# Layer 1's experts in a two-layer trunk: outputs added into DRAM by accumulating DMA, token rows taken for two experts by one f32 product, freed memory as weight slots

## The chip, the core and the metric

One core of one Trainium2 chip runs the whole program in one launch. The metric is the device time of an execution in microseconds (us), as the median of several. PE is TensorE, DVE VectorE, ACT ScalarE, POOL GpSimd, SP SyncE; a "record" is one matmul instruction as the profile counts it.

## The reference, cut to what matters

The program is a two-layer backbone for 256 latent tokens (and 256 context tokens, which layer 1 no longer updates) of width 1024. Each layer is a mixer and then a mixture of 16 experts; every token goes to 2 of them. The change is in layer 1's mixture (`need_ctx` is false there):

```python
y = merge(...)                                  # mixer, ends with @ w_out
x = x + m[:, :, 2] * y
h = rms_norm(x, norm2_g) * (1 + m[:, :, 4]) + m[:, :, 3]
g_logits = tf @ router_g                        # 4 groups, then 2 of 4 experts in the best group
...
for e in range(MOE_EXPERTS):                    # 16
    hid = jax.nn.silu(t @ w1[e]) * (t @ w3[e])  # 1024 -> 512
    out = out + gate[:, e:e + 1] * (hid @ w2[e])
x = x + m[:, :, 5] * out                        # the kernel's output
```

All of it is float32. The weights of one expert are w1 and w3 (1024 x 512 each) and w2 (512 x 1024): 6.3 MB.

## The kernel before, in words

**Weight stream.** Every weight goes through a chain of pieces of up to 1 MB (128 partitions x 2048 f32) on SP's DMA queue. `sources` fixes their order; layer 1's mixture has 96 pieces, "four of w1 and w3 of the next expert, two of w2 of this one". A piece lands in a slot of 8 KB per partition. `ws.take` hands the next piece to the compute code, `ws.done` gives its slot back, and `pump` (L159) at once issues the next load into a free slot; the load waits on SP until the last reader of that slot is done, and what comes later on SP waits behind it. `ws.add` turns free memory into slots wherever the program lets memory go. A separate chain for the modulation weights (`in_modw`) shares SP.

**Before the experts.** `finish` computes the end of the mixer: `out_half` (its matmuls are L331 to L333) gives x by column quarters, and a call-back `last` runs, for each quarter, `scaled` (L1300, x times the row A2, which is loaded at L469 on ACT's DMA queue from a small DRAM tensor `md`), `squares`, `logits` (transposes L1317, router products L1323) and `keep`, which splits the scaled row h into three bf16 parts (L1308 on ACT, L1310 on DVE or POOL). `halve` and `swap` give memory of the mixer to the slots. `moe` makes the routing: `rk` (a token's place in its expert's list), the gates `VAL` and the root mean square factor `rs`, both split in three bf16 parts.

**The experts, `experts_sum`.** Every expert has 64 places for tokens. `prepare(e)` makes the one-hot matrix of tokens by places and takes the expert's rows out of the 256 tokens: 48 bf16 matmuls (L1701: 8 blocks of columns, 2 tiles of tokens, 3 parts), 6 more for the row factor (L1693), and a DVE product and sum (L1704, L1706); it also turns the one-hots (L1708) and takes the gates (L1711). `first(e)` is the product with w1 and w3 (L1728, 64 records, two halves of the columns side by side in the PE array) and the SwiGLU; `second(e)` transposes the result (L1742), multiplies it with w2 (L1752, 16 records) and with the gates (L1758). The result y is split in two parts in bf16-like precision (L1761 on ACT, L1762 on DVE), and after every second expert 8 matmuls (L1767) add the rows of both experts back to their tokens, into four PSUM banks `acc` that hold the 256 x 1024 output all the time; they were seeded with x (L1684). The order of the program is prepare(e+1), first(e), second(e-1). At the end ACT and DVE copy `acc` out (L1782) and four DMAs store it (L1783). If an expert has over 64 tokens, `overflow` does the rest; it is a branch that these inputs don't take.

Layer 0's mixture has a piece that matters here: `scatter` (L1488) adds rows of y to rows of the DRAM tensor `yd` by an indirect DMA with addition, issued on POOL.

Of the kernel before, what the change touches and what calls it, by code (L numbers as in the profile page):

```python
# [16 lines left out]
P = 128  # L17
# [11 lines left out]
def _col_layout():  # L29
    off = 0  # L30
    for name, n in (("g1", 16), ("lcw", 16), ("lcb", 4), ("lba", 8), ("lbx", 8), ("lam", 8),
# [13 lines left out]
       "hot16": (1262, 16), "slot": (1278, 128), "dvc": (1406, 4)}  # L45
NMSK = 1410
# [205 lines left out]
class Trunk:  # L252
    def __init__(self, tc, I, out, es, dbg):
# [6 lines left out]
        self.es, self.wp, self.rp = es, ExitStack(), ExitStack()  # L260
# [100 lines left out]
    def setup(self):  # L361
# [894 lines left out]
    def finish(self, l, mix):  # L1256
# [24 lines left out]
        hb = F.get(2, 3, D, dt=BF) if ns == 1 else None  # L1281
        if ns == 2:

            H, self.hd = [F.get(2, D) for s in range(2)], self.dp.tile([4 * P, D], F32, name=f"hd{l}")
# [9 lines left out]
        hR = Ring(F, HR, 2, 256) if ns == 1 else None  # L1294
        wait, kept = ([], [], [], []), {}

        def scaled(c, s):
            sl = slice(256 * c, 256 * c + 256)
            h = kept[c, s] = hR() if ns == 1 else H[s][:, :, sl]
            nc.vector.tensor_tensor(h, self.X[s][:, :, sl], A2[:, s, sl].rearrange("p (o c) -> p o c", o=1)  # L1300
                                    .to_broadcast([P, 2, 256]), op=OP.mult)
# [30 lines left out]
        def last(c, s):  # L1332
            for i, f in enumerate((scaled, squares, logits, keep)):
# [6 lines left out]
        for i, f in enumerate((scaled, squares, logits, keep)):  # L1340
            for cs in wait[i]:
                f(*cs)
        F.free(*self.gates, junk, hfR, *([hR] if hR else []), rts, self.rt, A2)
# [10 lines left out]
        self.moe(l, H if ns == 2 else hb, lg)  # L1354
# [14 lines left out]
    def moe(self, l, hd, lg):  # L1369
# [85 lines left out]
        RV, r = F.get(nt, 3, dt=BF), [G_, T(1)[:, :, 0]]  # L1455
        for i in range(3):
            g_, s_ = (G, rs) if i == 0 else r
            nc.vector.tensor_copy(VAL[:, :, :, i], g_)
            if ns == 1:
                nc.vector.tensor_copy(RV[:, :, i], s_)  # L1460
            if i < 2:
                tt(r[0], g_, VAL[:, :, :, i], op=OP.subtract)
                if ns == 1:
                    tt(r[1], s_, RV[:, :, i], op=OP.subtract)
# [6 lines left out]
        else:  # L1471
            self.experts_sum(l, nt, hd, rk, G, VAL, RV, mxi)
            F.free(hd)
        F.free(rk, G, VAL, RV, rs, mxi)
# [190 lines left out]
    def experts_sum(self, l, nt, hb, rk, G, VAL, RV, mxi):  # L1665


        nc, I, F, R = self.nc, self.I, self.F, self.R
        G2 = F.get(2, 512)
        for o in range(2):  # L1670
            for c in range(2):
                r = slice(64 * (c ^ o), 64 * (c ^ o) + 64)
                nc.scalar.dma_start(G2[r, o], self.md[l, 2][0, c, 1:2].to_broadcast([64, 512]))
        ohR = Ring(F, 2, nt, P, dt=BF)
        gtR, xR, rsR = Ring(F, 3, 1), Ring(F, 2, KC, 64), Ring(F, 2, 64)
# [374 lines left out]
```

## Time and profile before

| | |
|---|---|
| time, median of 3 runs | 1256.99 us (1256.77 to 1258.33) |
| the profiled execution: its own time | 1263.97 us |
| its span in the trace | 1262.2 us |
| PE busy | 1109.3 us, 88% of the span |
| DVE, ACT, POOL busy | 806.6, 560.0, 340.6 us |
| DMA moved | 317.09 MB, mean 251 GB/s |

Times inside the program are us from the span's start. The experts of layer 1 take the last fifth, from about 1016 on. In the tables of stretches a row gives the length, busy time of PE, PEld (weight loads), DVE, ACT and POOL with their instructions, the granted clock of TensorE as a share of 2.4 GHz, the busy share of the 16 DMA engines and the rate in GB/s.

### The profile page before, as it was taken

To read this page: it belongs to the slowest core of one execution; us is meant where nothing else is said; L and a number is where in the kernel's file an instruction comes from. 1 tells how busy PE (TensorE), PEld (TensorE's weight loads), DVE (VectorE), ACT (ScalarE), POOL (GpSimd) and SP (SyncE) were. 2 spreads that over 40 slices of the span, in tenths; PEclk is the share of its full clock that TensorE was granted. 3 is DMA by queue.
4 is the path that set the end of the run, shared out by engine and by line. 5 is a ranking of instruction groups with operands and counts; after the bars stand their busy time and mean duration, and the time that the engine had idled before them with its cause. 6 is when DMAs were issued, how large, how long until landed. Compare 5 with 4: busy or idle time off the path is not lost. (4 is left out here: it accounts for less than half of the span.)

```text
span 1262.2 us, 18733 instructions
## 1 busy us (share of the span) xinstructions
PE 1109.3 (88%) x7206; PEld 780.4 (62%) x7206; DVE 806.6 (64%) x1376; ACT 560.0 (44%) x893; POOL 340.6 (27%) x214
## 2 busy tenths in 40 slices
PE   3998899999919999999999779988998599999996
PEld 1656665666717777777777356655777365555553
DVE  3576836555639999999898646998387533333232
ACT  3355525333417787887886323343353311111111
POOL 1331422233213444444532211344423200000000
PEclk9998988899959999999999888999998899999999
DMA  9663568266386999999983154343476789999960
GB/s 355 215 207 124 172 191 278 71 239 242 114 238 241 352 353 346 364 362 358 356 312 118 71 143 179 117 134 107 149 273 249 282 315 422 424 423 424 416 277 35
DMA packets 74977, 317.09 MB, mean 251 GB/s; under 512 B 20074, under 2 KB 26314, under 8 KB 46080
## 3 DMA queue, kind: packets, MB, share of 16 engines
q1 hardware_dynamic: 54656, 294.10, 61.4%
q0 software_dynamic: 4896, 10.20, 3.6%
q10 hardware_dynamic: 15328, 11.50, 3.3%
q8 instruction: 60, 0.98, 0.3%
q14 instruction: 37, 0.30, 0.1%
HBM read 310.74 MB, written 14.76 MB: 258 GB/s over the span
## 5 line engine op out<-in xcount | busy, mean ns | idle before, releaser
L322 ACT CAST arena_rw<-arena_f 128x1024 fp32r<-128x1024 f32 x256 | 265.1, 1050 | 177.7 <-PE b L333 111.3
L325 DVE TENSOR_TENSOR arena_rw<-arena_f,arena_rw 128x1024 fp32r<-128x1024 f32 x198 | 260.4, 1357 | 81.5 <-ACT arena_rw L322 80.9
L331 PE MATMUL b<-arena_rw,arena_rr 128*128 128x512 f32 (+1 forms) x736 | 275.1, 375 | 2.7 <-ACT arena_rr L1214 1.2
L332 PE MATMUL b<-arena_rw,arena_rr 128*128 128x512 f32 (+1 forms) x736 | 272.0, 370 | 0.0
L333 PE MATMUL b<-arena_rw,arena_rr 128*128 128x512 f32 (+1 forms) x736 | 270.1, 369 | 0.5 <-DVE arena_rr L1215 0.5
L325 POOL TENSOR_TENSOR arena_rw<-arena_f,arena_rw 128x1024 fp32r<-128x1024 f32 x58 | 144.4, 2490 | 235.8 <-ACT arena_rw L322 220.6
L331 PEld LDWEIGHTS b<-arena_rw,arena_rr 128*128 128x128 f32 x736 | 140.5, 191 | 37.9 <-issue 10.6
L333 PEld LDWEIGHTS b<-arena_rw,arena_rr 128*128 128x128 f32 x736 | 140.0, 191 | 25.6 <-issue 3.3
L332 PEld LDWEIGHTS b<-arena_rw,arena_rr 128*128 128x128 f32 x736 | 140.7, 191 | 21.2 <-issue 1.3
L417 PE MATMUL b<-arena_f,cs 128*32 128x256 f32 x768 | 70.2, 420 | 22.2 <-DMA arena_f<-in_modw 22.0
L331 PE MATMUL b<-arena_rr,arena_rw 128*128 128x512 f32 (+1 forms) x192 | 74.4, 391 | 2.7 <-ACT arena_rw L322 1.4
L1728 PE MATMUL b<-arena_f 128*64 128x256 f32 x656 | 76.0, 381 | 0.0
L333 PE MATMUL b<-arena_rr,arena_rw 128*128 128x512 f32 (+1 forms) x192 | 72.3, 380 | 4.1 <-DVE arena_rw L325 4.1
L332 PE MATMUL b<-arena_rr,arena_rw 128*128 128x512 f32 (+1 forms) x192 | 73.6, 384 | 1.0 <-POOL arena_rr L507 1.0
L1728 PEld LDWEIGHTS b<-arena_f 128*64 128x64 f32 x656 | 46.5, 137 | 24.2 <-issue 2.3
L417 PEld LDWEIGHTS b<-arena_f,cs 128*32 128x32 f32 x768 | 20.8, 113 | 56.3 <-issue 26.8
L1761 ACT CAST arena_rr<-arena_f 64x512 fp32r<-64x512 f32 x32 | 19.8, 618 | 69.7 <-DVE arena_f L1758 69.3
L1733 ACT ACTIVATE arena_f<-b 128x256 f32<-128x256 f32 x16 | 6.2, 385 | 98.0 <-PE b L1728 98.0
L331 PEld LDWEIGHTS b<-arena_rr,arena_rw 128*128 128x128 f32 x192 | 36.7, 192 | 18.2 <-issue 7.4
L1744 DVE COPY arena_f<-b 128x256 f32<-128x256 f32 x16 | 6.8, 424 | 64.1 <-PE b L1742 64.0
L1488 POOL DMA_INDIRECT yd<-arena_f x14 | 33.5, 2390 | 50.5 <-ACT arena_f L1578 50.5
L553 POOL TENSOR_TENSOR arena_f<-arena_f 128x512 f32<-128x512 f32 x21 | 30.5, 1458 | 57.1 <-DVE arena_f L550 54.8
(386 smaller groups left out, 1798.2 us busy)
## 6 DMA issues: line engine op xcount, KB each, us to landing
arena_f<-in_moe SPq DMA_DIRECT2D x192, 1024.0 KB
arena_f<-in_modw SPq DMA_DIRECT2D x96, 512.0 KB
arena_f<-in_wod SPq DMA_DIRECT2D x18, 1024.0 KB
arena_f<-in_wev SPq DMA_DIRECT2D x14, 1024.0 KB
arena_f<-md ACTq DMA_DIRECT2D x8, 512.0 KB
arena_f<-in_tok SPq DMA_DIRECT2D x4, 512.0 KB
yd<-arena_f SPq DMA_DIRECT2D x4, 512.0 KB
hd<-md ACTq DMA_DIRECT2D x4, 512.0 KB
```

Source lines behind the costliest of these rows:

```text
L322: nc.scalar.copy(h, raw)
L325: eng.tensor_tensor(l, raw, h.bitcast(F32), op=OP.subtract)
L331: nc.tensor.matmul(ps, ah, bh, start=first, stop=False)
L332: nc.tensor.matmul(ps, ah, bl, start=False, stop=False)
L333: nc.tensor.matmul(ps, al, bh, start=False, stop=last)
L417: nc.tensor.matmul(acc[32 * i:32 * i + 32, 0:256], self.cs[:, k, :], raw[:, i * 256:(i + 1) * 256], start=(k == 0), stop=(k == KC - 1))
L553: (nc.vector if last and c == 3 else nc.gpsimd).tensor_tensor(xs, xs, tmp, op=OP.add)
L1488: self.nc.gpsimd.indirect_dma_start(out=yd[:, :], out_offset=bass.IndirectOffsetOnAxis(ap=dst, axis=0), in_=y, in_offset=None, bounds_chec ...
L1728: nc.tensor.matmul(p[64 * c:64 * c + 64, 256 * w:256 * w + 256], x[:, 4 * b + k], raw[:, 512 * k + 256 * c:512 * k + 256 * c + 256], start ...
L1733: nc.scalar.activation(u, p[:, 0:256], AF.Tanh, scale=0.5)
L1744: nc.vector.tensor_copy(ut, ps[:, 0:256].rearrange("p (b c) -> p b c", b=2))
L1761: nc.scalar.copy(yh[r, c], y[r])
```

## The change

`experts_sum` is written anew:

- The output is no longer gathered in PSUM. x goes to `out` by two DMAs ahead of the experts (L1662, ACT's queue); then each expert's y (128 half rows of 512 f32, 2 KB each) is added into `out`, seen as 512 half rows, by one accumulating indirect DMA on POOL (`scatter`, now L1479). The places' destinations and gates come from `rows(e)`: four bf16 matmuls with 2 or 3 columns (L1681, L1683) and two small DVE instructions.
- `take(j)` takes the rows of experts 2j and 2j+1 with one f32 one-hot, already multiplied by the row factor: 4 DVE instructions build it (L1694), 16 f32 matmuls of 128x128x128 (L1700, two records each) make x for both, and 2 DVE instructions add the shift (L1702). H stays whole in f32: `keep`, its bf16 parts, `RV`, L1693, L1704, L1708, the split of y and L1761, L1762, L1767, L1684, L1782 and L1783 are gone.
- `first` is cut in two around w1 and w3, and `hidden(e-1)` (the transposes), `take` and `rows` stand in between. The copy of the transposes goes from DVE to ACT.
- Memory: without the bf16 parts one more slot is added at the start of `finish`; `swap` also closes `rr2` and gives 2 slots (`F4`); the PSUM-side buffers in `RW` are gone; X[0] is freed as soon as it is copied to `out`. Followed through the program, the largest number of slots in layer 1's mixture goes from 16 to 19. Each load into memory that was X[0] has to wait for the DMAs of L1662.

```diff
+        self.vi2 = cp.tile([P, 4, 2], BF, name="vi2")
+        nc.gpsimd.tensor_tensor(self.vi2, self.vi, self.vi, op=OP.add)
         self.ss, junk = F.get(4, 2), F.get(512, dt=BF)
-        hb = F.get(2, 3, D, dt=BF) if ns == 1 else None
+        H = [F.get(2, D) for s in range(ns)]
...
-        def keep(c, s):
-            sl, h = slice(256 * c, 256 * c + 256), kept.pop((c, s))
-            if ns == 2:
-                return
-            for i in range(3):
-                nc.scalar.copy(hb[:, :, i, sl], h)
-                if i < 2:
-                    (nc.gpsimd if HP[c] else nc.vector).tensor_tensor(h, h, hb[:, :, i, sl], op=OP.subtract)
...
     def halve(self):
         self.rp.close()
-        self.R = self.arena(self.es, "rr2", NR // 2, F32R, "right")
         self.F3 = self.arena(self.es, "f3", NR // 2, F32, "right")
+        self.R = self.arena(self.rq, "rr2", NR // 2, F32R, "right")
         self.ws.add(NR // 4096, self.F3)
     def swap(self):
+        self.rq.close()
+        self.F4 = self.arena(self.es, "f4", NR // 2, F32, "right")
+        self.ws.add(NR // 4096, self.F4)
         self.wp.close()
         self.F2 = self.arena(self.es, "f2", 2048 * NHL)
         self.ws.add(NHL, self.F2)
...
-    def experts_sum(self, l, nt, hb, rk, G, VAL, RV, mxi):
...
+    def experts_sum(self, l, nt, H, rk, rs, G, VAL, mxi):
+        nc, I, F = self.nc, self.I, self.F
+        half = self.out.rearrange("t (c d) -> (t c) d", c=2)
+        for t in range(nt):
+            nc.scalar.dma_start(self.out[t * P:(t + 1) * P, :], self.x(t))
+        G2 = F.get(512)
+        for c in range(2):
+            nc.scalar.dma_start(G2[64 * c:64 * c + 64], self.md[l, 2][0, c, 1:2].to_broadcast([64, 512]))
+        ohR, phR = Ring(F, 3, nt, P, dt=BF), Ring(F, 2, nt, P)
+        gtR, ddR, xR = Ring(F, 6, 1), Ring(F, 6, 1, dt=I32), Ring(F, 2, KC, P)
-        uR, utR, yR = Ring(F, 2, 256), Ring(F, 2, 2, P), Ring(F, 2, 512)
-        sR, yhR, ylR = Ring(R, 2, 2, nt * P), Ring(R, 1, 2, 512), Ring(R, 1, 2, 512)
+        uR, utR, yR = Ring(F, 2, 256), Ring(F, 2, 2, P), Ring(F, 3, 512)
+        F.free(self.X[0])
-        acc = [[self.bank("a") for c in range(2)] for t in range(nt)]
-        for t in range(nt):
-            for c in range(2):
-                nc.tensor.matmul(acc[t][c], self.ident, self.x(t)[:, 512 * c:512 * c + 512], start=True, stop=False)
-        st = {}
-        def prepare(e):
...
             for t in range(nt):
-                for i in range(3):
-                    nc.tensor.matmul(tb[:, 320:384], RV[:, t, i:i + 1].to_broadcast([P, P]), oh[:, t, 0:64],
-                                     start=(t == 0 and i == 0), stop=(t == nt - 1 and i == 2))
-            rr = rsR()
-            nc.scalar.copy(rr, tb[:, 320:384])
-            ps = self.bank()
-            for k in range(KC):
-                for t in range(nt):
-                    for i in range(3):
-                        nc.tensor.matmul(ps[:, 64 * k:64 * k + 64], hb[:, t, i, k * P:(k + 1) * P], oh[:, t, 0:64],
-                                         start=(t == 0 and i == 0), stop=(t == nt - 1 and i == 2))
-            x = xR()
-            nc.vector.tensor_tensor(x, ps.rearrange("p (k t) -> p k t", k=KC),
-                                    rr.rearrange("p (o t) -> p o t", o=1).to_broadcast([P, KC, 64]), op=OP.mult)
-            nc.vector.tensor_tensor(x, x, shift.to_broadcast([P, KC, 64]), op=OP.add)
...
+        st, xs, us = {}, {}, {}
+        def rows(e):
             oh = ohR()
             self.one_hot(oh, "slot", rk, e)
             tb = self.bank()
             for t in range(nt):
+                nc.tensor.matmul(tb[:, 0:2], oh[:, t], self.vi2[:, t], start=(t == 0), stop=(t == nt - 1))
             for t in range(nt):
+                nc.tensor.matmul(tb[:, 2:5], oh[:, t], VAL[:, t, e], start=(t == 0), stop=(t == nt - 1))
+            gt, dst = gtR(), ddR()
+            nc.vector.tensor_scalar(dst, tb[:, 0:1], tb[:, 1:2], self.msk("dsc"), op0=OP.add, op1=OP.add)
+            nc.vector.tensor_reduce(gt, tb[:, 2:5], AX.X, OP.add)
+            st[e] = gt, dst
+        def take(j):
+            ph, x = phR(), xR()
             for t in range(nt):
+                for o in range(2):
+                    nc.vector.tensor_scalar(ph[:, t, 64 * o:64 * o + 64], self.msk("slot")[:, 0:64],
+                                            rk[:, t, 2 * j + o:2 * j + o + 1], rs[:, t:t + 1], op0=OP.is_equal, op1=OP.mult)
+            for b in range(2):
+                ps = self.bank()
+                for k in range(4):
+                    for t in range(nt):
+                        nc.tensor.matmul(ps[:, k * P:(k + 1) * P], H[:, t, (4 * b + k) * P:(4 * b + k + 1) * P], ph[:, t],
+                                         start=(t == 0), stop=(t == nt - 1))
+                nc.vector.tensor_tensor(x[:, 4 * b:4 * b + 4], ps.rearrange("p (k t) -> p k t", k=4),
+                                        shift[:, 4 * b:4 * b + 4].to_broadcast([P, 4, P]), op=OP.add)
+            xs[2 * j], xs[2 * j + 1] = x[:, :, 0:64], x[:, :, 64:128]
...
+                if w == 0:
+                    u = uR()
+                    nc.scalar.activation(u, p[:, 0:256], AF.Tanh, scale=0.5)
+                    nc.vector.scalar_tensor_tensor(u, u, 1.0, p[:, 0:256], op0=OP.add, op1=OP.mult)
+                yield
...
+        def hidden(e):
+            u, ps, ut = us[e], self.bank(), utR()
             for b in range(2):
                 nc.tensor.transpose(ps[:, b * P:(b + 1) * P], u[:, b * P:(b + 1) * P], self.ident)
-            ut = utR()
-            nc.vector.tensor_copy(ut, ps[:, 0:256].rearrange("p (b c) -> p b c", b=2))
-            py = self.bank("m")
+            nc.scalar.copy(ut, ps[:, 0:256].rearrange("p (b c) -> p b c", b=2))
+            us[e] = ut
...
             y = yR()
-            yh, yl = yhR(), ylR()
-            nc.vector.scalar_tensor_tensor(y, py, gt, G2[:, e % 2], op0=OP.mult, op1=OP.mult)
-            for i in range(2):
-                r, c = slice(64 * i, 64 * i + 64), i ^ e % 2
-                nc.scalar.copy(yh[r, c], y[r])
-                nc.vector.tensor_tensor(yl[r, c], y[r], yh[r, c].bitcast(F32), op=OP.subtract)
-            if e % 2:
-                for i, part in enumerate((yh, yl)):
-                    for t in range(nt):
-                        for c in range(2):
-                            nc.tensor.matmul(acc[t][c], S[:, c, t * P:(t + 1) * P], part[:, c], start=False,
-                                             stop=(e == NE - 1 and i == 1))
-        prepare(0)
+            nc.vector.scalar_tensor_tensor(y, py, gt, G2, op0=OP.mult, op1=OP.mult)
+            self.scatter(half, y, dst)
+        take(0)
+        rows(0)
         for e in range(NE + 1):
-            if e < NE - 1:
-                prepare(e + 1)
-            if e < NE:
-                first(e)
+            f = first(e) if e < NE else iter(())
+            next(f, None)
+            if e:
+                hidden(e - 1)
+            if e % 2 and e < NE - 1:
+                take(e // 2 + 1)
+            if e + 1 < NE:
+                rows(e + 1)
+            run_all(f)
             if e:
                 second(e - 1)
-        F.free(ohR, gtR, xR, rsR, uR, utR, yR, G2)
-        for t in range(nt):
-            for c in range(2):
-                sl = slice(512 * c, 512 * c + 512)
-                (nc.vector.tensor_copy if c else nc.scalar.copy)(self.x(t)[:, sl], acc[t][c])
-                (nc.sync if c else nc.scalar).dma_start(self.out[t * P:(t + 1) * P, sl], self.x(t)[:, sl])
-        R.free(sR, yhR, ylR)
+        F.free(ohR, phR, gtR, ddR, xR, uR, utR, yR, G2)
...
+    put("dsc", 2 * BIG + k // 64)
```

In the rows below, one of PE, of before, in the loop (expert 2): `arena_f` is the common f32 memory of tokens, one-hots and weight slots, `b_...` a PSUM bank, the last word the shape of the output and "x8" the number of equal rows. Left of the arrow is what is written.

```order
L1693 MATMUL b_8360<-arena_f 128x64
L1708 LDWEIGHTS arena_f
L1708 MATMUL b_8360<-bfs,arena_f 128x128
L1752 MATMUL b_8335<-arena_f_6980,arena_f 64x512 x4
L1752 MATMUL b_8335<-arena_f_7550,arena_f 64x512 x4
L1701 LDWEIGHTS arena_f
L1701 MATMUL b_8368<-arena_f 128x64
```

Of the changed kernel, PE at the first pass of the loop, from the end of w1 of expert 0:

```order
L1714 MATMUL b_7694<-arena_f 64x256 x11
L1729 MATMUL b_7715<-mskt,arena_f 128x128 x2
L1700 MATMUL b_7723<-arena_f 128x128 x8
L1700 MATMUL b_7733<-arena_f 128x128 x8
L1681 LDWEIGHTS arena_f
L1681 MATMUL b_7744<-vi_99,arena_f 128x2
```

and, a few rows on, from the end of `rows(1)` to the start of expert 2:

```order
L1683 MATMUL b_7744<-arena_f 128x3
L1714 MATMUL b_7694<-arena_f 64x256 x16
L1741 MATMUL b_7770<-arena_f 64x512 x8
L1714 MATMUL b_7785<-arena_f 64x256 x8
L1714 MATMUL b_7785<-arena_f_6978,arena_f 64x256 x8
L1729 MATMUL b_7806<-mskt,arena_f 128x128 x2
```

Between L1742's turn and w2 stood 48 bf16 products per expert and now none; ahead of w3 stand 16 f32 products for two experts.

On SP, the loads in the last part of layer 1's mixer, of before (`in_wod` are pieces of the mixer's weights, `in_modw` of the modulation, `in_moe` of layer 1's experts):

```order
L159 DMA arena_f<-in_modw 128x1024 x2
L159 DMA arena_f<-in_wod 128x2048
L159 DMA arena_f<-in_modw 128x1024 x2
L159 DMA arena_f<-in_wod 128x2048
L159 DMA arena_f<-in_modw 128x1024
L159 DMA arena_f<-in_wod 128x2048
L159 DMA arena_f<-in_modw 128x1024
L159 DMA arena_f_6980<-in_wod 128x2048
L159 DMA arena_f<-in_modw 128x1024
L159 DMA arena_f_6980<-in_moe 128x2048
```

and the same place now:

```order
L159 DMA arena_f<-in_modw 128x1024
L159 DMA arena_f<-in_moe 128x2048
L159 DMA arena_f<-in_modw 128x1024
L159 DMA arena_f<-in_wod 128x2048
L159 DMA arena_f<-in_modw 128x1024 x2
L159 DMA arena_f<-in_wod 128x2048
L159 DMA arena_f<-in_moe 128x2048
L159 DMA arena_f<-in_modw 128x1024
L159 DMA arena_f<-in_wod 128x2048
L159 DMA arena_f<-in_modw 128x1024
L159 DMA arena_f_6978<-in_wod 128x2048
```

Two pieces of the experts moved ahead of the last mixer pieces; the order inside each chain is the same.

On POOL, which had nothing to do in layer 1's experts before, the first of the 16 scatters (512x512 is `out` as half rows), with the semaphores that each waits for (DMASW... is that of an earlier scatter, DMAHW... of a load or store of a hardware queue):

```order
L1479 DMA out<-arena_f 512x512 [waits DMAHW1_49,DMAHW3_49,DMAHW0_49,DVE_49]
L1479 DMA out<-arena_f 512x512 [waits DMASW2_49,DMASW3_49,DVE_49,Activation_49]
L1479 DMA out<-arena_f 512x512 [waits DMASW3_49,DVE_49,Activation_49]
L1479 DMA out<-arena_f 512x512 [waits DMASW5_49,DMASW4_49,DVE_49]
L1479 DMA out<-arena_f 512x512 [waits DMASW5_49,DVE_49]
```

Each scatter waits for the one before it to have landed and for DVE's product with the gates.

## Rows read from the trace of the kernel before

**Rows 1.** Busy time by stretch: the experts, and PE after the weights.
```profile
1020.00:1220.00 200.00, 191.96 (x2018) 113.62 (x2016) 63.33 (x117) 35.48 (x93) 0.00 (x0) 1.00 1.01 418
1220.00:1255.00 35.00, 31.24 (x200) 15.48 (x196) 12.32 (x21) 6.28 (x12) 0.00 (x0) 1.00 0.03 14
```

**Rows 2.** Chain that ended last, in the experts: start, duration, what.
```profile
1016.57 7.06 PE b L1728 x64
...
1081.64 0.73 PE b L1767 x2
1082.45 1.49 PE b L1767 x6
...
1092.48 3.58 PE b L1752 x16
1096.07 1.51 PE b L1701 x48
...
1111.07 0.73 PE b L1767 x2
...
1250.98 0.76 DVE arena_f L1758
...
1252.49 2.08 PE b L1767 x7
```

**Rows 3.** Waits of SP's queue, 1020 to 1221: total us, times, longest.
```profile
SPq L159 <- PE b L1728: 101.7, 42, 5.7
```

**Rows 4.** Groups by line, one pair of experts (1081.64 to 1111.07): busy, mean ns, idle.
```profile
L1742 PE MATMUL b<-mskt,arena_f 128*128 128x128 f32 x4 | 0.9, 300 | 0.0
L1708 PE MATMUL b<-bfs,arena_f 128*128 128x128 bf16 x4 | 0.9, 218 | 0.7 <-ACT arena_f L1696 0.7
L1693 PE MATMUL b<-arena_f 128*128 128x64 bf16 x12 | 0.7, 193 | 0.0
L1711 PE MATMUL b<-arena_f 128*128 128x1 bf16 x12 | 0.6, 164 | 0.0
```

**Rows 5.** The same chain in the mixer: 8 f32 products of 128x128x128.
```profile
902.71 1.78 PE b L1168 x16
```

**Rows 6.** Layer 0's scatters on POOL: duration, first and last start, landing.
```profile
L1488 POOL DMA_INDIRECT yd<-arena_f x14: 1897/2504/2527, 412.1 to 661.6; - x14
DMA to landing us min/median/max: 6.6/11.2/11.5
```

**Rows 7.** DMA queues, 560 to 640, four scatters and four gathers: packets, MB, share.
```profile
DMA packets 4874, 28.84 MB, mean 361 GB/s; under 512 B 1056, under 2 KB 1056, under 8 KB 1658
q0 software_dynamic: 1253, 2.47, 13.4%
```

**Rows 8.** Loads on SP's queue ahead of A2's, by time: start, us, count.
```profile
972.70 2.41 SPq L159 DMA_DIRECT2D arena_f<-in_moe  x5
```

**Rows 9.** The same chain, from A2's load to the first expert.
```profile
974.98 13.05 DMA arena_f<-md
...
1000.22 2.58 PE b L1684 x6
...
1011.36 2.57 PE b L1701 x48
```

**Rows 10.** Waits of SP's queue, 960 to 1020.
```profile
SPq L159 <- PE b L333: 21.9, 1, 21.9
```

**Rows 11.** Busy time by stretch, around the routing.
```profile
974.00:988.00 14.00, 8.98 (x74) 8.57 (x72) 2.31 (x7) 1.62 (x5) 2.24 (x2) 0.97 0.98 393
988.00:998.00 10.00, 4.89 (x24) 4.08 (x25) 5.56 (x9) 5.42 (x12) 5.88 (x4) 0.52 0.05 21
998.00:1013.50 15.50, 8.90 (x85) 5.37 (x84) 12.31 (x65) 6.83 (x17) 0.07 (x1) 0.81 1.00 372
1013.50:1019.50 6.00, 5.84 (x106) 4.77 (x105) 3.25 (x6) 1.91 (x7) 0.00 (x0) 0.91 0.05 10
```

**Rows 12.** Waits of SP's queue at the end, after its last store.
```profile
SPq L1835 <- SPq L1835: 4.2, 2, 3.6
```

**Rows 13.** SP's and ACT's last stores, by time: start, us, count.
```profile
1254.89 0.91 SPq L1783 DMA_DIRECT2D out<-arena_f  x2
1255.21 2.27 ACTq L1783 DMA_DIRECT2D out<-arena_f  x2
```

More of the change, by code (lines that the diff above doesn't have):

```diff
@@ L44 @@
        "colm": (937, 64), "pidx": (1001, 1), "cneg": (1002, 128), "cnegT": (1130, 128), "hot4": (1258, 4),
-       "hot16": (1262, 16), "slot": (1278, 128), "dvc": (1406, 4)}
-NMSK = 1410
+       "hot16": (1262, 16), "slot": (1278, 128), "dvc": (1406, 4), "dsc": (1410, 1)}
+NMSK = 1411
 class Arena:
@@ L1279, in finish @@
         self.ss, junk = F.get(4, 2), F.get(512, dt=BF)
-        hb = F.get(2, 3, D, dt=BF) if ns == 1 else None
+        H = [F.get(2, D) for s in range(ns)]
         if ns == 2:
-            H, self.hd = [F.get(2, D) for s in range(2)], self.dp.tile([4 * P, D], F32, name=f"hd{l}")
+            self.hd = self.dp.tile([4 * P, D], F32, name=f"hd{l}")
             for s in range(2):
@@ L1332, in last @@
         def last(c, s):
-            for i, f in enumerate((scaled, squares, logits, keep)):
+            for i, f in enumerate((scaled, squares, logits)):
                 wait[i].append((c, s))
@@ L1339, in finish @@
         run_all(self.out_half(l, 1, mix, ns, last))
-        for i, f in enumerate((scaled, squares, logits, keep)):
+        for i, f in enumerate((scaled, squares, logits)):
             for cs in wait[i]:
                 f(*cs)
-        F.free(*self.gates, junk, hfR, *([hR] if hR else []), rts, self.rt, A2)
+        F.free(*self.gates, junk, hfR, rts, self.rt, A2)
         self.R.free(*mix)
@@ L1471, in moe @@
         else:
-            self.experts_sum(l, nt, hd, rk, G, VAL, RV, mxi)
-            F.free(hd)
-        F.free(rk, G, VAL, RV, rs, mxi)
+            self.experts_sum(l, nt, hd[0], rk, rs, G, VAL, mxi)
+            F.free(hd[0])
+        F.free(rk, G, VAL, rs, mxi)
     def one_hot(self, out, name, rk, e):
@@ L1703, in prepare @@
-            x = xR()
-            nc.vector.tensor_tensor(x, ps.rearrange("p (k t) -> p k t", k=KC),
-                                    rr.rearrange("p (o t) -> p o t", o=1).to_broadcast([P, KC, 64]), op=OP.mult)
-            nc.vector.tensor_tensor(x, x, shift.to_broadcast([P, KC, 64]), op=OP.add)
-            for t in range(nt):
-                nc.tensor.matmul(tb[:, t * P:(t + 1) * P], oh[:, t], self.identb, start=True, stop=True)
-            for t in range(nt):
-                for i in range(3):
-                    nc.tensor.matmul(tb[:, 256:257], oh[:, t], VAL[:, t, e, i:i + 1], start=(t == 0 and i == 0),
-                                     stop=(t == nt - 1 and i == 2))
@@ L1786, in xt @@
         def xt(xT, ohb, oh, cols):
-            ps, rr = self.bank(), F.get(P)
+            ph = F.get(nt, P)
             for t in range(nt):
-                for i in range(3):
-                    nc.tensor.matmul(ps[:, 0:P], RV[:, t, i:i + 1].to_broadcast([P, P]), ohb[:, t],
-                                     start=(t == 0 and i == 0), stop=(t == nt - 1 and i == 2))
-            nc.scalar.copy(rr, ps[:, 0:P])
+                nc.vector.tensor_scalar(ph[:, t], oh[:, t], rs[:, t:t + 1], None, op0=OP.mult)
@@ L1796, in xt @@
                     for t in range(nt):
-                        for i in range(3):
-                            nc.tensor.matmul(ps[:, k * P:(k + 1) * P], hb[:, t, i, (4 * b + k) * P:(4 * b + k + 1) * P],
-                                             ohb[:, t], start=(t == 0 and i == 0), stop=(t == nt - 1 and i == 2))
-                xb = xT[:, 4 * b:4 * b + 4]
-                nc.vector.tensor_tensor(xb, ps.rearrange("p (k t) -> p k t", k=4),
-                                        rr.rearrange("p (o t) -> p o t", o=1).to_broadcast([P, 4, P]), op=OP.mult)
-                nc.vector.tensor_tensor(xb, xb, shift[:, 4 * b:4 * b + 4].to_broadcast([P, 4, P]), op=OP.add)
-            F.free(rr)
+                        nc.tensor.matmul(ps[:, k * P:(k + 1) * P], H[:, t, (4 * b + k) * P:(4 * b + k + 1) * P], ph[:, t],
+                                         start=(t == 0), stop=(t == nt - 1))
+                nc.vector.tensor_tensor(xT[:, 4 * b:4 * b + 4], ps.rearrange("p (k t) -> p k t", k=4),
+                                        shift[:, 4 * b:4 * b + 4].to_broadcast([P, 4, P]), op=OP.add)
+            F.free(ph)
         def put(y, oh, cols):
-            G2, S = F.get(D), F.get(nt, P)
+            G2, pd, dst = F.get(D), self.bank(), F.get(1, dt=I32)
             self.mod_row(G2, l, 5, 0)
-            ps = self.bank()
             for t in range(nt):
-                nc.tensor.transpose(ps[:, t * P:(t + 1) * P], oh[:, t], self.ident)
-            nc.vector.tensor_copy(S, ps[:, 0:nt * P].rearrange("p (t c) -> p t c", t=nt))
-            for c in range(2):
-                sl = slice(512 * c, 512 * c + 512)
-                nc.vector.tensor_tensor(y[:, sl], y[:, sl], G2[:, sl], op=OP.mult)
-                for t in range(nt):
-                    ps = self.bank()
-                    nc.tensor.matmul(ps, S[:, t], y[:, sl], start=True, stop=True)
-                    nc.vector.tensor_tensor(self.x(t)[:, sl], self.x(t)[:, sl], ps, op=OP.add)
-            F.free(G2, S)
+                nc.tensor.matmul(pd[:, 0:1], oh[:, t], self.msk("dvc")[:, t:t + 1], start=(t == 0), stop=(t == nt - 1))
+            nc.vector.tensor_scalar(dst, pd[:, 0:1], BIG, None, op0=OP.add)
+            nc.vector.tensor_tensor(y, y, G2, op=OP.mult)
+            self.scatter(self.out, y, dst)
+            F.free(G2, dst)
         u, y = F.get(512), F.get(D)
@@ L1877, in overflow @@
                     put(y, oh, cols)
-            if l:
-                for t in range(nt):
-                    nc.sync.dma_start(self.out[t * P:(t + 1) * P, :], self.x(t))
         F.free(w, *cols, r2, oh, ohb, gt, xT, uT)
```

56 lines of the change are left out of this document (16 added, 40 removed).

## Prediction

> **What bounds the kernel now.** I read the stretches first [rows 1]. Between 1020 and 1220 PE is busy 191.96 of 200 us, and the 16 DMA engines are just as full (share 1.01, 418 GB/s). Then the weights end, and PE works on alone for 35 us with DMA at 0.03. So the two are close, and PE is behind. Which of them holds the other is seen in the waits of SP's queue [rows 3]: in 201 us its loads wait 101.7 us for a matmul of L1728 to give back a slot. The loads are fast enough, and the slots are full of weights that PE has not used. The end is therefore set by when PE starts on the experts and by its time per expert.
>
> The chain [rows 2] gives both. PE starts L1728 at 1016.57; L1767 comes every 29.43 us (1081.64, 1111.07), which is a pair of experts, 14.7 each; PE's last matmul ends at 1254.57 (1252.49 and 2.08). Then come 7.6 us of copies and stores.
>
> **The sum, PE.** A pair now, from the rows: L1728 2 x 7.06, L1752 2 x 3.58, L1767 2.22 (0.73 and 1.49), L1701 2 x 1.51 [rows 2]; the transposes 0.9, L1708 0.9 and 0.7 of waiting, L1693 0.7, L1711 0.6 [rows 4]. With overlap that is 29.4. What goes: 3.02, 2.22, 0.9, 0.7, 0.7, 0.6, about 8.1, of which some 0.7 overlaps in the pipeline: 7.4. What comes: `take`, 16 f32 products. The mixer has the same product at the same shape: 8 of them, 16 records, 1.78 us at full clock [rows 5], so 32 records are 3.6. And `rows`, 2 x 4 narrow bf16 products; L1711's 12 took 0.6 [rows 4], so 0.4. A pair is then 29.4 - 7.4 + 4.0 = 26.0, 13.0 per expert. The copies, the split and the sums on DVE and ACT that go lay beside PE, and what stays there (0.8 us on ACT for two transposes' copies, and DVE's small steps) has over 2 us of `take`, `rows` and w3 in front of its reader; if that cover is gone it costs at most the 0.7 that L1708 waited. Sixteen experts are 208, less the first `take`, which lies before the start: 204.5. I add 2 for stalls.
>
> **The start.** Three things move it.
> (1) The row A2 is loaded at 974.98 and lands 13.05 later [rows 9]. Five pieces of the experts were issued between 972.70 and 975.1 [rows 8], and DMA was full until 988 [rows 11]: 5.2 MB at 393 GB/s are 13.3 us, so the small load landed with the last of them. PE then idles and its clock is 0.52 until 998 [rows 11]. With the extra slot the changed program issues two pieces of the experts earlier, ahead of mixer pieces, so three or four stand before A2 instead of five. I take 4.6 us (between 1 x 2.5 and 3 x 2.5, a piece being 1.05 MB at 418 GB/s); the bounds are 0 and 7.5.
> (2) L1684 (2.58 us at 1000.22 [rows 9]) and the bf16 casts and subtractions of `keep` and RV leave the routing: 2.6.
> (3) `take(0)` makes two experts, 3.6 us at full clock and 7.1 at half; L1701 for the first expert took 2.57 there instead of 1.51 [rows 9, 2], so the clock is low. With four DVE instructions in front I charge 1.2 more than L1693 and L1701 of both took. Net of (2) and (3): 1.4 earlier.
> Start: 1016.57 - 4.6 - 1.4 = 1010.6. PE ends at 1010.6 + 204.5 + 2 = 1217.
>
> A rule speaks against (1). The Trainium skill's page "DMA: Bandwidth & Descriptors", section "Queues, rings and completion order", says that each DMA engine goes round the queues that have work for it, packet by packet. By it A2, on ACT's queue, would not stand behind SP's five pieces, and having fewer of them ahead would give little. The 13.05 us [rows 9] look rather like a line; by the rule the start is 1015.2, which is rival A.
>
> **The sum, weights.** PE can't be faster than the stream. SP waited 21.9 us for L333, until 997 [rows 10], with its slots full; by the program 11 pieces of this mixture had been issued then, and 12 are in the changed one, where I put this point at 992. Left are 84 pieces of 2.51 us: 210.8. The store of x adds 2.5 (1.05 MB at 418). The scatters add 512 rows of 4 KB, 2.1 MB; in layer 0 that queue's transfers, 2.47 MB, took 13.4% of 80 us [rows 7], 230 GB/s, so 9.1. At 1013.5 to 1019.5 DMA idled (0.05 [rows 11]) because slots were full before PE began; with 19 slots instead of 16 about 2.4 of that stays. Last landing: 992 + 210.8 + 2.5 + 9.1 + 2.4 = 1217, then 1.9 for the last half of w2: 1219. Both sums meet; I take 1218.
>
> **The tail.** After the last matmul: DVE's product 0.75 [rows 2], then scatters 14 and 15, one after the other. Layer 0's took from 6.6 (the last one, beside idle DMA) to 11.5 from issue to landing [rows 6]. With idle DMA: number 14 is issued about 3.5 before PE's end and lands 3.1 after it, number 15 lands 6.6 later, 9.7. From the landing to the span's end 3: SP waited 3.6 after its last store was issued at 1255.8 [rows 12, 13], 1259.4, and the span ends at 1262.2. So 12.7 in place of 7.6.
>
> Span: 1218 + 12.7 = 1230.7, 31.5 less than 1262.2. The profiled execution's own time, 1263.97, is 7.0 above the median, so I subtract from the median: **1225.5 us**.
>
> The skill's same page, section "Anatomy of one DMA - SWDGE (gpsimd) path", gives 2.0 us and bytes / 436 GB/s for such a transfer. By it a scatter of 256 KB is 2.6 us (an estimate from that page), the tail about 6.4 and the time 1219. The traced scatters, of twice the bytes, took 6.6 at least [rows 6], and I keep to them.
>
> **Rivals.**
> A. *A2 lands no earlier.* For it: it is on another queue. Against it: it landed just when the pieces ended. Start 1015.2, PE's end 1222, span 1234.5, time 1229.
> B. *The scatters are dearer to the stream.* An addition in DRAM reads what it writes; if 2.1 MB cost 18 us, not 9, the last piece lands at 1226 and the span is 1240, the time 1235. For it: DMA is full in this stage; against it, the same kind of transfer in [rows 7].
> C. *The scatters stand in line behind weight pieces.* If a scatter waits for what SP issued before it, as A2 did, its landing grows by 2.5 with each piece ahead, and with fast PE many slots are free and their loads in line. Above 13.0 us the chain of scatters (each waits for the one before) is slower than PE; y's three buffers then hold PE back to the stream's pace, about 15.5 per expert, until the pieces end. The first scatter starts at 1033 (start and 22 us), so some 12 have landed by 1213, four more at 6.9 each end at 1241, the span is 1244 and the time 1239. For it: 11.2 in layer 0 against 6.6 when idle [rows 6].
> D. *Slower.* The same chain, if every scatter, also those beside idle DMA, takes over 14.1: 1033 + 16 x 14.1 + 3 = 1262. From there the kernel is slower than before; at 15.5 it is 1284 and the time 1279. Against it: 11.5 was the longest of 14, with twice the bytes a row [rows 6]. That the scatters must not overlap at all is in the skill's same page, "Rules for kernel authors": an accumulating transfer beside another access of the same bytes loses additions, so the earlier one's semaphore has to be waited for. The program does so.
> E. *PE isn't faster.* If the f32 product runs at half clock in the loop (7.1 per pair), a pair is 29.5 as before, PE ends at 1241 (1010.6 + 236 - 7.1 + 2), the span is 1254 and the time 1249. Against it: the clock is 1.00 in this stage [rows 1].
>
> **Chances and range.** My forecast 0.47 (1219 to 1228), A 0.15, B 0.12, C 0.18, D 0.05, E and others 0.03. The lower bound: start 1007.5 with A2 7.5 earlier, no stalls, the scatters at 418 GB/s: PE's end 1212, and a tail of 10.3 if number 14 has landed by then, so 1222 and 1217. The upper bound takes in C: 1241. A measurement of this kernel can tell about 0.2%, 2.5 us, from no change; faster by more than that 0.93, within it 0.02, slower 0.05.
>
> **What would show it.** Right: L1714's starts in the profile of the changed kernel 26.0 apart per pair, L1700's 32 records at 3.6, the first at about 1011; A2's load 8 to 9 us instead of 13; POOL's L1479 with 6.6 to 11.5 from issue to landing and never the releaser of DVE's L1746; DMA at 1.0 to the end of the experts. Wrong: pairs longer than 27 with L1746 waiting for a scatter (C, D), PE waiting for `in_moe` pieces in the middle of the experts (B), or the first L1714 at 1015 (A).

## The result

The changed kernel takes 1240.64 us (1239.45 to 1246.33, 4 runs) against 1257.66 for the kernel before on the same chip: 17.0 us less, ratio 0.9861, 95% interval 0.9814 to 0.9909. In a second series it was 0.9844 (0.9803 to 0.9885). The forecast was 1225.5, so the direction was right and little over half of the gain came. The time lies 0.4 us below the upper end of the stated range (1217 to 1241); that end was set for rival C, which did not happen, so it is luck that the range holds. Executions of one program differ here by up to 14 us (1230.80 to 1244.35 in the second series of the changed kernel), and part of it comes long before layer 1: layer 0's first router product starts at 329.3 us in the profile of before, at 320.8 in that of the changed kernel and at 331.5 in that of the run order_kept. What a step takes is therefore read inside the stage, from the issue of A2's load on.

### The profile page after: what moved, and what is told of

Read it like the earlier page. It is cut to its first block, busy times and chain, and to the rows that moved or that the text cites. A ratio compares the mean times of both kernels' runs of the same rounds, so it can differ in the third digit from the quotient of the medians.

```text
span 1239.5 us, 17204 instructions
## 1 busy us (share of the span) xinstructions
PE 1088.7 (88%) x6462; PEld 775.7 (63%) x6462; DVE 776.1 (63%) x1363; ACT 520.4 (42%) x799; POOL 360.9 (29%) x229
## 5 line engine op out<-in xcount | busy, mean ns | idle before, releaser
L1479 POOL DMA_INDIRECT out<-arena_f x16 | 24.9, 1557 | 220.7 <-DVE arena_f L1746 216.8
L1714 PE MATMUL b<-arena_f 128*64 128x256 f32 x608 | 72.2, 381 | 4.5 <-DVE arena_f L1721 4.5
L1714 PEld LDWEIGHTS b<-arena_f 128*64 128x64 f32 x608 | 47.2, 137 | 26.8 <-DVE arena_f L1721 6.4
L1714 PE MATMUL b<-arena_f,arena_f 128*64 128x256 f32 x416 | 49.9, 381 | 1.9 <-DVE arena_f L1721 1.9
L1479 POOL DMA_INDIRECT yd<-arena_f x14 | 32.0, 2284 | 52.0 <-ACT arena_f L1569 52.0
L1474 POOL DMA_INDIRECT arena_f<-hd,arena_f x16 | 27.3, 1706 | 64.1 <-DVE arena_f L1514 50.5
```

The lines of the kernel that those rows point to most:

```text
L1474: self.nc.gpsimd.indirect_dma_start(out=xg, out_offset=None, in_=hd[:, :], in_offset=bass.IndirectOffsetOnAxis(ap=tk, axis=0), bounds_chec ...
L1479: self.nc.gpsimd.indirect_dma_start(out=yd[:, :], out_offset=bass.IndirectOffsetOnAxis(ap=dst, axis=0), in_=y, in_offset=None, bounds_chec ...
L1714: nc.tensor.matmul(p[64 * c:64 * c + 64, 256 * w:256 * w + 256], x[:, 4 * b + k], raw[:, 512 * k + 256 * c:512 * k + 256 * c + 256], start ...
```

## The profile after

Busy time by stretch of the changed kernel, columns as in [rows 1]:
```profile
1020.00:1220.00 200.00, 188.96 (x1467) 117.21 (x1465) 44.44 (x116) 11.30 (x30) 21.80 (x14) 1.00 0.99 402
1220.00:1240.00 20.00, 8.19 (x42) 2.62 (x38) 1.93 (x3) 0.37 (x1) 3.10 (x2) 0.77 0.17 21
```
PE and DMA are both full, as before. The DMA share falls in this kernel between 1212 and 1220, shown below beside another kernel. Yet PE's last matmul starts at 1226.83.

The start and the scatters. A2's load is issued at 972.48, and L1301, which waits for it, starts at 982.35; the first matmul of the experts (L1714) starts at 1009.77. Scatters on POOL, by time: start, duration, and what ended the idle time before:
```profile
1033.14 1.58 POOL L1479 DMA_INDIRECT out<-arena_f  x1 [45.35 <-DVE arena_f L1746]
1045.48 1.56 POOL L1479 DMA_INDIRECT out<-arena_f  x1 [10.76 <-DVE arena_f L1746]
1059.99 1.56 POOL L1479 DMA_INDIRECT out<-arena_f  x1 [12.95 <-DVE arena_f L1746]
...
1112.69 1.55 POOL L1479 DMA_INDIRECT out<-arena_f  x1 [12.97 <-DVE arena_f L1746]
...
1141.15 1.55 POOL L1479 DMA_INDIRECT out<-arena_f  x1 [14.67 <-DVE arena_f L1746]
1156.12 1.55 POOL L1479 DMA_INDIRECT out<-arena_f  x1 [13.41 <-DVE arena_f L1746]
...
1201.13 1.55 POOL L1479 DMA_INDIRECT out<-arena_f  x1 [13.48 <-DVE arena_f L1746]
1213.75 1.55 POOL L1479 DMA_INDIRECT out<-arena_f  x1 [11.06 <-DVE arena_f L1746]
1226.36 1.55 POOL L1479 DMA_INDIRECT out<-arena_f  x1 [11.06 <-DVE arena_f L1746]
1231.80 1.55 POOL L1479 DMA_INDIRECT out<-arena_f  x1 [3.88 <-DMA out<-arena_f]
```
From 1033.14 to 1112.69 are six experts, 13.26 each; from 1141.15 to 1201.13 it is 15.0 each, and 12.6 in the two after that, which have no `take` left. Only the last scatter waits for its predecessor; all others wait for DVE's product, so for PE. In this stage they take, from issue to landing:
```profile
DMA to landing us min/median/max: 4.7/8.6/9.7
```

Why an expert gets longer is seen in PE's timeline. An early stretch with `take` (start, duration, line, records):
```profile
1047.31 0.44 PE L1729 MATMUL b<-mskt,arena_f 128*128 128x128 f32 x2
1047.59 3.74 PE L1700 MATMUL b<-arena_f 128*128 128x128 f32 x32
1051.16 0.19 PE L1681 MATMUL b<-vi,arena_f 128*128 128x2 bf16 x2
1051.21 0.19 PE L1683 MATMUL b<-arena_f 128*128 128x3 bf16 x2
1051.33 1.95 PE L1714 MATMUL b<-arena_f 128*64 128x256 f32 x16
1053.11 1.90 PE L1714 MATMUL b<-arena_f,arena_f 128*64 128x256 f32 x16
1054.84 3.60 PE L1741 MATMUL b<-arena_f 128*64 128x512 f32 x16
1058.27 3.62 PE L1714 MATMUL b<-arena_f 128*64 128x256 f32 x32
```
an early one without `take`:
```profile
1036.34 0.64 PE L1741 MATMUL b<-arena_f,arena_f 128*64 128x512 f32 x1 [0.38 <-ACT arena_f L1730]
1036.67 0.43 PE L1714 MATMUL b<-arena_f,arena_f 128*64 128x256 f32 x1
1036.82 0.59 PE L1741 MATMUL b<-arena_f,arena_f 128*64 128x512 f32 x1
```
and late ones:
```profile
1148.93 0.83 PE L1700 MATMUL b<-arena_f 128*128 128x128 f32 x6
1149.70 1.94 PE L1741 MATMUL b<-arena_f 128*64 128x512 f32 x8
1151.57 1.60 PE L1700 MATMUL b<-arena_f 128*128 128x128 f32 x12
...
1166.41 3.65 PE L1741 MATMUL b<-arena_f,arena_f 128*64 128x512 f32 x16
1169.89 3.62 PE L1714 MATMUL b<-arena_f,arena_f 128*64 128x256 f32 x32
1174.45 3.67 PE L1714 MATMUL b<-arena_f,arena_f 128*64 128x256 f32 x32 [0.94 <-DVE arena_f L1721]
1178.65 0.44 PE L1729 MATMUL b<-mskt,arena_f 128*128 128x128 f32 x2 [0.52 <-DVE arena_f L1723]
1178.92 0.83 PE L1700 MATMUL b<-arena_f 128*128 128x128 f32 x6
```
Early, in a pass with `take`, PE runs in the order of the code: the transposes of the expert before, `take` and `rows` stand between w1 and w3, and nothing waits. In the early passes without `take` w2 and w3 are mixed record by record, and PE waits 0.4 to 0.7 us for ACT's copy of the transposes (L1730). Late, w3 follows w1 at once and waits 0.94 us for DVE's L1721, which reads w1's half of the same PSUM bank; and the transposes follow w3 at once and wait 0.52 for DVE's L1723, their own input. PE's instructions are laid out when the program is built, so this is its order, not an accident of the run (no_scatter, below, has the same waits): from about the tenth expert on the built program has w1 and w3 in one piece in every second expert, and in the others `take` cut in pieces among w2 and the first half of w1. All of PE's waits from 1015 to the end (us in total, times, longest):
```profile
PE b L1714 <- DVE arena_f L1721: 6.3, 7, 0.9
PE b L1729 <- DVE arena_f L1723: 3.7, 7, 0.5
PE b L1741 <- ACT arena_f L1730: 1.6, 3, 0.7
```
No wait for a piece is among them; the weight loads (PEld), which lie beside PE's matmuls, show 1.5 us of such waits. On the other side SP, from 1100 to 1215, no longer waits for PE, as in [rows 3], but for its own loads:
```profile
SPq L159 <- DMA arena_f<-in_moe: 85.4, 38, 3.5
...
SPq L159 <- PE b L1714: 1.0, 3, 0.4
```
So the stream ran at full speed with slots to spare. Its loads thin out from 1212 on, and the last packets land at about 1218.5 (SP's queue moves 0.01 MB from 1218 to 1219 and nothing after it); PE ended 10 us after that, at 1228.72.

## Experiments

**Theory 1:** PE's laid order is the bound; its waits for DVE and ACT cost the 11.6 us of the rows above and some 3 more for the pieces into which `take` is cut. **Theory 2** (rival B in a wider form): the stream is the bound, since 15.0 us an expert is also about what six pieces and a scatter need at 410 to 420 GB/s. The times inside the stage come from PE's timeline (first and last matmul of the experts) and ACT's (issue of A2's load); "again" is a second run.

| kernel | A2's issue to start | start to PE's end | PE's end to span's end | ratio to before of the same series (95%) |
|---|---|---|---|---|
| before | 41.5 | 238.3 | 7.4 | 1 |
| changed | 37.3 | 219.0 | 10.8 | 0.9861 (0.9814, 0.9909) |
| changed, again | 36.8 | 219.0 | 10.2 | 0.9844 (0.9803, 0.9885) |
| order_kept | 35.8 | 212.0 | 8.8 | 0.9779 (0.9728, 0.9831) |
| two_banks | 36.4 | 211.4 | 8.7 | 0.9777 (0.9723, 0.9830) |
| both | 36.5 | 211.6 | 9.1 | 0.9800 (0.9761, 0.9839) |
| both, again | 35.9 | 211.9 | 8.9 | 0.9796 (0.9753, 0.9839) |
| no_scatter | 36.2 | 219.0 | 1.9 | 0.9773 (0.9698, 0.9847) |
| late_slot | 38.5 | 220.7 | 10.4 | 0.9839 (0.9770, 0.9908) |
| slots16 | 37.2 | 221.3 | 10.7 | 0.9874 (0.9824, 0.9924) |
| both_slots16 | 36.9 | 218.7 | 8.9 | 0.9799 (0.9754, 0.9845) |
| both_slots16, again | 36.6 | 218.6 | 8.9 | 0.9859 (0.9812, 0.9905) |
| only_scatter | 40.0 | 218.7 | 10.1 | 0.9874 (0.9829, 0.9918) |

**order_kept.** The same instructions, PE's held in the order of the code:
```diff
+        def chained():
+            return self.tc.issue_after(pe[0].ins) if pe[0] else ExitStack()
...
-                    for k in range(4):
-                        for c in range(2):
-                            nc.tensor.matmul(p[64 * c:64 * c + 64, ...
+                    with chained():
+                        for k in range(4):
+                            for c in range(2):
+                                last = nc.tensor.matmul(p[64 * c:64 * c + 64, ...
+                    pe[0] = last
```
(and so for `rows`, `take`, `hidden` and `second`; some lines of the code are cut short).

> The changed kernel with PE's instructions of the experts held in the order in which the code is written (each block issued behind the last matmul of the one before), nothing else. Theory 1 (PE's order): from about 1125 us on the laid order puts w3 straight behind w1 and the transposes straight behind w3, so PE waits 0.94 and 0.52 us per expert and loses about 1 us more per pair by changing back and forth; an expert then takes 15.0 us, and PE ends 13.7 us behind the last weight. In the order of the code a pair keeps its early 26.4 us to the end, PE ends at 1217 to 1219, span 1228 to 1230, 9 to 12 us faster than the changed kernel. Theory 2 (the stream): DMA is full (share 1.0) and one expert's pieces and its scatter need 15.0 us, so PE is paced by its weights whatever its order: within 2 us of the changed kernel, the gaps turn up as waits for pieces.

Start to PE's end went from 219.0 to 212.0, the ratio from 0.9861 to 0.9779 (the intervals overlap a little, so the gain is read from the stage). From 207 to 209 was expected. PE's waits, from 1015 on:
```profile
PE b L1722 <- DVE arena_f L1730: 6.7, 9, 1.1
PE b L1753 <- SPq L1815: 1.2, 3, 0.6
PE b L1722 <- SPq L1815: 0.7, 1, 0.7
PE b L1753 <- ACT arena_f L1741: 0.5, 1, 0.5
PE b L1722 <- DMA arena_f<-in_moe: 0.4, 1, 0.4
```
(L1722, L1730, L1753 and L1741 are the changed kernel's L1714, L1721, L1741 and L1730; L1815 is SP's branch to `overflow`): every second expert has no `take` between w1 and w3, and its wait is still 0.7; but the wait on the transposes is gone and `take` is in one piece. In the last 20 us PE waits for pieces too, 2.3 us: the waits put down to SP's branch are read as such, since each stands ahead of the first record on a new piece.

Take all these waits off, and PE's part is 207.4 us in the changed kernel (219.0 less 11.6) and 202.5 here (212.0 less 9.5). By this count the order in which PE's work stands gave 4.4 us on the waits for DVE and ACT and 4.9 on work that is no longer cut and mixed, which shows in no wait, and 2.3 went to pieces. PE's order was the bound. The stream lay 7 us behind it: the last loads land about 209 us after the start in the changed kernel and 210 here, and PE ends here 2 us after them.

**two_banks.** w3's product gets a bank of its own, and nothing holds PE's order:
```diff
-            p = self.bank("a")
+            p2 = [self.bank("a"), self.bank("a")]
             for w in range(2):
+                p = p2[w]
...
-            py = self.bank("a")
+            py = self.bank("m")
```


> The changed kernel with w1's and w3's products in two PSUM banks instead of two halves of one (w2's product goes to another bank for that), nothing else; the laid order stays. Theory 1: w3 no longer waits for DVE's L1721; the 0.94 us go in each of the 7 experts that show it, 6 to 7 us faster than the changed kernel (span 1233). Theory 2: no change, within 2 us.

211.4, 7.6 less. Of the three waits one is left:
```profile
PE b L1730 <- DVE arena_f L1724: 4.2, 8, 0.5
```
(L1730 and L1724 are L1729 and L1723 of the changed kernel); 2.1 us of others come in the last 20 us, where the last pieces land. The late passes stand as in the changed kernel, but the builder laid the early ones without `take` anew, w2 no longer mixed with w3, so the 7.6 are not the bank's alone. Theory 2, which expected nothing of either edit, falls.

**no_scatter.** The call of `scatter` in `second` is left out, so the output is x alone.
```diff
-            self.scatter(half, y, dst)
```


> The changed kernel without the 16 scatters: the experts' results are computed and not added to the output, which is x alone. Theory 1: PE goes at its own pace, so its last matmul stays at 1228 to 1229 although the stream has 2.1 MB less; only the tail goes, span 1232 (7 us faster). The weights land about 8 us earlier. Theory 2: the stream is 8 us shorter and PE with it, and the tail goes too: span 1224 (15 us faster).

PE's part is 219.0 to the tenth, with 2.1 MB less to move: the surest sign that the stream did not pace PE. The weights end earlier. The changed kernel, then this one, whose start lies 2.5 us later (columns as in [rows 1]):
```profile
1208.00:1212.00 4.00, 3.48 (x18) 1.26 (x18) 0.42 (x1) 0.37 (x1) 0.00 (x0) 1.00 0.95 397
1212.00:1216.00 4.00, 4.00 (x36) 2.30 (x32) 0.75 (x1) 0.00 (x0) 1.55 (x1) 1.00 0.57 231
1216.00:1220.00 4.00, 3.06 (x30) 2.00 (x30) 0.42 (x1) 0.39 (x1) 0.00 (x0) 1.00 0.23 67
```
```profile
1204.00:1208.00 4.00, 3.06 (x30) 1.81 (x28) 0.42 (x1) 0.38 (x1) 0.00 (x0) 1.00 0.94 387
1208.00:1212.00 4.00, 3.48 (x30) 1.89 (x28) 0.42 (x1) 0.28 (x1) 0.00 (x0) 1.00 0.19 78
1212.00:1216.00 4.00, 4.00 (x26) 1.67 (x24) 0.74 (x1) 0.10 (x1) 0.00 (x0) 1.00 0.00 0
```
Taking the falling shares as the ends, about 1215 and 1208.6, they lie 205.2 and 196.3 after the start; by the last packets of SP's queue (about 1218.5 and 1210.7) it is 209 and 198. So the scatters cost the stream 9 to 10 us; the sum had 9.1.

**late_slot.** The extra slot at the end of the mixer is given back only later.
```diff
-        self.ws.add(F.fits(2048) - FA[l])
+        self.ws.add(F.fits(2048) - FA[l] - l)
```


> The changed kernel with the extra slot of the mixer's end given to the stream only later, as before (7 in place of 8 there). Theory on A2: five pieces of the experts stand again ahead of the load of row A2, it lands 3 to 5 us later in relation to the mixer's end, the first expert's first matmul starts at 1013 to 1015 instead of 1009.8, and the time is 3 to 5 us longer. Rival: the load on ACT's queue does not stand in line, the start stays within 1 us and so does the time.

L1301 starts 11.2 us after A2's issue (971.44 to 982.66) instead of 9.9, and the first expert 38.5 instead of 37.3. So one slot is worth 1.3 us there by this pair, where 3 to 5 was expected; the rival's bound of 1 us is nearly met. The size is rough: in the ten runs that have the slot L1301 starts 9.5 to 10.8 us after A2's issue, and in the two whose mixer has the slots of before, before and only_scatter, 13.1 and 12.1. The time, 0.9839 of before, shows nothing.

**both.** Order and banks together.

> The changed kernel with PE's order held as the code is written and with two banks for w1's and w3's products, together. With either alone PE came to wait for pieces at the end, and the stream ended with PE. If the stream is now the bound, both together bring little over one of them: first matmul of the experts to PE's last 208 to 212 us (211.6 with either alone, 219.0 in the changed kernel), the time 10 to 13 us under the changed kernel's. If PE's order were still the bound: 5 us more, 204 to 206 from start to end.

211.6, as with either alone: as expected of a stream that has become the bound. PE's waits:
```profile
PE b L1723 <- DMA arena_f<-in_moe: 4.0, 6, 1.2
PE b L1723 <- SPq L1816: 1.3, 2, 1.1
PE b L1754 <- SPq L1816: 1.3, 3, 0.6
PE b L1754 <- DVE arena_f L1733: 0.6, 1, 0.6
PE b L1754 <- ACT arena_f L1742: 0.5, 1, 0.5
PE b L1754 <- DMA arena_f<-in_moe: 0.5, 1, 0.5
```
(L1723 and L1754 are the changed kernel's L1714 and L1741; L1816 is SP's branch, read as above.) Now PE waits for pieces, 7.1 us, and hardly for DVE and ACT. The time, 0.9800 of before against 0.9861, is some 8 us under the changed kernel's, where 10 to 13 was expected; the intervals overlap.

**slots16 and both_slots16.** The changed kernel, and `both`, with three slots fewer:
```diff
-        self.ws.add(NR // 4096, self.F4)
...
-        F.free(self.X[0])
```


> The changed kernel with 16 slots instead of 19: F4 and X[0] are not given to the stream. Theory 1 (PE's order is the bound in the changed kernel): the three slots hold pieces that PE doesn't miss; start to PE's end 219 to 222 us, the time within 3 us of the changed kernel. Theory 2 (the stream is the bound): three pieces later, 7.5 us slower.

> As both, with 16 slots instead of 19. Here the stream is the bound, so the same three slots should now cost: the last piece lands later by up to three pieces of 2.5 us, 4 to 8 us slower than both. If the slots had no part in it, within 2 us of both.

In the changed kernel three slots are worth 2.3 us inside the stage; in `both`, 7.1. The first times of the second pair said otherwise (0.9800 and 0.9799), so changed, both and both_slots16 ran once more side by side.

> The changed kernel once more, beside the two below on one chip. Start to PE's end 219 us; the ratio to before 0.984 to 0.990.

> PE's order as written and two banks, once more. By the traces so far: start to PE's end 211 to 212, tail 9, so 9 us under the changed kernel of the same chip (0.9922 of it).

> The same with 16 slots, once more: its trace showed 7.1 us more from start to PE's end, its time none. If the trace is right (the stream is the bound and the three slots cost 2.4 us each), 4 to 8 us over both_again; if the time is right, within 2 us of it.

The stage repeated itself (219.0, 211.9, 218.6), and the medians came out at 1238.48, 1234.71 and 1240.47: the slots' 5.8 us are there, as in the stage (6.7), though the intervals overlap; in the first pair the two profiled executions are 9.7 us apart already at A2's issue (974.35 and 964.66), which hides such a difference. `both` was 3.8 us under the changed kernel in this series, where 9 was expected; the intervals (0.9753 to 0.9839 and 0.9803 to 0.9885) overlap, and the stage shows 8.4 with the tail (7.1 and 1.3).

**only_scatter.** The kernel before, with the change's output part alone:
```diff
+        for t in range(nt):
+            nc.scalar.dma_start(self.out[t * P:(t + 1) * P, :], self.x(t))
...
-                nc.tensor.matmul(tb[:, t * P:(t + 1) * P], oh[:, t], self.identb, start=True, stop=True)
+                nc.tensor.matmul(tb[:, 0:2], oh[:, t], self.vi2[:, t], start=(t == 0), stop=(t == nt - 1))
...
-            yh, yl = yhR(), ylR()
+            self.scatter(half, y, dst)
```
(L1684, L1716, L1761 to L1767, L1782 and L1783 go.)

> The kernel before with the output part of the change alone: x stored to the output first, y added by the 16 scatters, so that L1767, its split on ACT and DVE, L1708 and L1684 go; the rows are still taken by 48 bf16 products per expert from three parts, and 16 slots stay. By the sum PE's pair loses 2.2 (L1767), 0.9 and 0.7 (L1708 and its wait) and gains 0.2: 25.8 to 26.2 a pair, as good as with the f32 product (3.0 and 0.6 against 3.6), so most of the change's gain is this part: start to PE's end 208 to 214 if the stream with 16 slots lets it (about 216 if not), the start at most 3 us earlier than before, the time 1235 to 1242. If the f32 product is what matters, the time stays within 6 us of before.

0.9874: all of the changed kernel's gain, as far as the intervals tell. Its scatters start at 1031.28, 1044.64, 1058.00, so a pair takes 26.7 (25.8 to 26.2 was expected), and from 1126 on 27.3. Start to PE's end is 218.7, above the 216 expected at most and the same as `both` with 16 slots: what 16 slots let the stream do. The last loads land 216 to 217 us after the start in slots16, both_slots16 and only_scatter, and 209 to 210 in the changed kernel, order_kept, two_banks and `both`, whatever PE's order. With 16 slots the f32 product gained nothing in PE's part: slots16, which has it in the laid order, takes 221.3. The start is 40.0 from A2's issue, 1.5 earlier than before; the other 2.7 of the changed kernel's 4.2 belong to its other parts, by single runs.

Not tried: the f32 product alone in the kernel before, and a laid order other than these three.

## Why the prediction was right or wrong

- **PE's sum: right but for one term.** 32 records of L1700 take 3.57 us in the loop (1047.59 to 1051.16), forecast 3.6; rival E falls. The early pairs are 26.5, forecast 26.0. **The step that failed is "I add 2 for stalls".** 204.5 without stalls has become 219.0: 14.5, of which 11.6 are the waits shown, 9.3 of them waits that only the late order has; the rest is work that is cut and mixed. The rows of PE's order ahead of the prediction are those of the first passes, where `take` stands between w1 and w3, and I took them for all sixteen. There was a warning: the text beside them says that in the kernel before 48 bf16 products stood between the transposes and w2, but its rows have only L1693 and L1708 there, which the builder had moved ahead of w2, and the 48 behind it (L1752 at 1092.48, L1701 at 1096.07 in [rows 2]). So the order of the code did not hold in that kernel either. order_kept and two_banks show what the term was worth: 7.0 and 7.6, with the stream as the bound after that. None of the listed signs of being wrong fits: pairs became 30 us long, and L1746 waited for PE alone.
- **The stream's sum: right.** Forecast 1217 for the last landing, traced about 1218.5, with 9 to 10 us for the scatters (9.1 in the sum). Rival B (dearer scatters) falls. That both sums would meet came true only where the order or the banks were mended: in order_kept, two_banks and `both` PE ends about 2 us after the last load, as the sum's 1.9 had it.
- **The start: right in total by luck, too much on A2.** 1010.6 forecast, 1009.77 traced; but the execution was 2.5 us early already at A2's issue. From there the gain is 4.2, not 6.0: A2's wait gave 3.2 of the 4.6, and the rest about 1.0 of the 1.4. Of rival A, that A2 doesn't land earlier, late_slot leaves a part: a slot gave 1.3, and runs of like programs differ there by about 1.
- **The tail: sign right, size too large.** 10.8 against 12.7, since a scatter beside idle DMA lands in 4.7 and not 6.6. The estimate of 2.6 for it by the Trainium skill's page "DMA: Bandwidth & Descriptors", section "Anatomy of one DMA - SWDGE (gpsimd) path", is too low for this indirect, adding transfer: the measurement decides.
- **Rivals C and D** fall: SP issued its last load at 1198.5, and it landed at about 1218.5, so some 20 us of loads were on their way, and the scatters still landed within 9.7. They didn't stand in line behind SP's pieces, and only the last one ever waited for its predecessor. The rule of the Trainium skill's page "DMA: Bandwidth & Descriptors", section "Queues, rings and completion order", that each DMA engine goes round its queues, agrees with these 8.6 us.
- The forecast in one line: 31.5 less; the stage gave 20.1 in the profile (start 4.2, PE 19.3, tail -3.4), the times 17.0 (11.4 to 23.4 by the interval). The 0.2% that I took a measurement to tell was too fine: the interval is 0.5% to either side.

## What to carry to other kernels

Where a builder lays out the instructions, read the order in the late passes of a loop too: one bank shared by two products is free while other work stands between them, and costs a round trip through ACT and DVE (0.94 us here) in each pass when the layout moves that work. What is lost where products are cut and mixed shows in no wait (some 4.9 us here); it takes a run with the order held to see it. Two engines that show the same pace are not yet one cause: take work from one of them and see whether the other moves. And a resource that is freed (here three slots) pays only when its user is the bound: 2.3 us in the changed kernel, 7.1 when PE's order was mended.

## What the runs showed of the hardware

Scatters with addition of up to 128 rows of 2 KB (1.39 MB in 11 of them, so 126 KB each: only places with a token are written) landed in 8.6 us (median of 16, most of them beside a full stream) and in 4.7 beside an idle one, and 16 of them held the weight loads up by 9 to 10 us. What they add to the end is that of the last two: PE's end to the span's end is 10.8 us, against 1.9 without scatters. I had expected 6.6 for the idle case.
